# A row gradient in 32 tiles: every third store moved to Pool's DMA queue, in two halves

## The chip, the core and the metric

The kernel runs on one core of a Trainium2 chip. The metric is the device time in microseconds (us) of one execution; the profile's span, from the first to the last instruction, is a little shorter. Of the core's engines the kernel uses VectorE (DVE in the profile), GpSimd (POOL), and SyncE (SP) for issuing DMA transfers. The core has 16 DMA engines, which carry out all transfers between the main memory (DRAM) and the on-chip memory with its 128 partitions (SBUF).

## The reference

```python
def reference(x: np.ndarray) -> np.ndarray:
    return np.gradient(x, axis=1)
```

x is 8192 x 8192 in float32, 268.4 MB, and so is the output. Inside a row the gradient is half the difference of the right and the left neighbour; the first element is x[1] - x[0] and the last is x[-1] - x[-2].

## The kernel before

A tile is 256 rows: 128 partitions with R = 2 rows each, so one partition holds 64 KB that lie together in DRAM, and a tile is 8.39 MB. There are 32 tiles. NB = 3 slots in SBUF hold one tile each; tile i lives in slot i % 3. A slot has SH = 64 spare columns at its front: the load (line 60) puts the tile behind them, and the result is written into the same slot 64 columns further to the front, so that no second buffer is needed.

Per tile the steps are:

1. The load, on SP's queue (line 60). From the fourth tile on it waits until the store of the tile that had the slot before has landed.
2. Pool takes the differences at both ends of each row into `ends` (line 70). It waits for the load.
3. VectorE works out the inside of both rows in one custom instruction, half the difference of two shifted views (line 81). It waits for step 2. The last tile is done in two pieces.
4. The end values are copied over the row ends of the result (line 92), by VectorE, or by Pool for tiles with i % 5 equal to 1 or 3.
5. The store, on SP's queue (line 94). It waits for step 4.

The order on each engine is written by hand (`manual_schedule`), and every engine works through its own list in order. SP's list is: loads of tiles 0 to 2; then, for each group of three tiles, their three stores and after them the three loads of the next group. A wait at the head of SP's list therefore holds up all that stands behind it. The helper `chain` names for each instruction the steps that it has to wait for; `stores[i]` is what the load of tile i + 3 waits for:

```python
ins = nc.sync.dma_start(out=b[:, SH : SH + W], in_=x_sets[i])
loads.append(chain(i, ins, *([stores[i - NB]] if i >= NB else [])))
```

Of the kernel before, what the change touches and what calls it, by code (L numbers as in the profile page):

```python
# [1 line left out]

# [4 lines left out]


@with_exitstack
def kernel(  # L10
    ctx: ExitStack,
    tc: tile.TileContext,
    x: bass.AP,
    out: bass.AP,
):

    nc = tc.nc
    P = nc.NUM_PARTITIONS
    n, m = x.shape
    R = 2
    NB = 3  # L30
    SH = 64
    W = R * m
    nsets = n // (P * R)
    f32 = x.dtype

    x_sets = x.rearrange("(s p t) m -> s p (t m)", p=P, t=R)
    out_sets = out.rearrange("(s p t) m -> s p (t m)", p=P, t=R)

    pool = ctx.enter_context(tc.tile_pool(name="pool", bufs=1))
    slots = [pool.tile([P, SH + W], f32, name=f"slot{k}", tag=f"slot{k}") for k in range(NB)]  # L40
    ends = pool.tile([P, nsets, R, 2], f32, name="ends", tag="ends")
    loads, stores = [], [None] * nsets
    in_front = {}

    def chain(i, ins, *needed):

        group, engine = f"slot{i % NB}", ins.ins.engine
        keep = [o.ins for o in needed]  # L50
        if in_front.get(engine, (None,))[0] == group:
            keep.append(in_front[engine][1])
        tc.declare_no_dep(ins.ins, group=group, keep=keep, reason="implied by the needed step")
        tc.add_to_no_dep_group(group, ins.ins)
        in_front[engine] = group, ins.ins
        return ins

    def load(i):
        b = slots[i % NB]
        ins = nc.sync.dma_start(out=b[:, SH : SH + W], in_=x_sets[i])  # L60
        loads.append(chain(i, ins, *([stores[i - NB]] if i >= NB else [])))

    with tc.manual_schedule():
        for i in range(NB):
            load(i)
        for i in range(nsets):
            b = slots[i % NB]
            xin = b[:, SH : SH + W].rearrange("p (t m) -> p t m", m=m)

            ins = nc.gpsimd.tensor_sub(  # L70
                out=ends[:, i, :, :],
                in0=xin[:, :, 1 : m : m - 2],
                in1=xin[:, :, 0 : m - 1 : m - 2],
            )
            at = [chain(i, ins, loads[i])]
            last = i == nsets - 1
            nr = 1 if last else R
            for r in range(0, R, nr):
                c0, c1 = r * m + 1, (r + nr) * m - 1

                ins = nc.vector._custom_dve(  # L81
                    dve_ops.TENSOR_TENSOR_REDUCE_SUB_MAX,
                    out=b[:, c0:c1],
                    in0=b[:, SH + c0 + 1 : SH + c1 + 1],
                    in1=b[:, SH + c0 - 1 : SH + c1 - 1],
                    s0=0.0,
                    s1=0.5,
                )
                halved = chain(i, ins, *at)
                res = b[:, r * m : (r + nr) * m].rearrange("p (t m) -> p t m", m=m)  # L90
                placer = nc.gpsimd if i % 5 in (1, 3) and not last else nc.vector
                ins = placer.tensor_copy(out=res[:, :, 0 : m : m - 1], in_=ends[:, i, r : r + nr, :])  # L92
                placed = chain(i, ins, halved)
                ins = nc.sync.dma_start(
                    out=out_sets[i, :, r * m : (r + nr) * m], in_=b[:, r * m : (r + nr) * m]
                )
                stores[i] = chain(i, ins, placed)
                at = [halved]
            if i % NB == NB - 1:
                for k in range(i + 1, min(i + 1 + NB, nsets)):  # L100
                    load(k)


# [1 line left out]
_INS = ['x']  # L105
_OUTS = [((8192, 8192), 'float32')]


# [23 lines left out]
```

## Time and profile before

| | before |
|---|---|
| device time, median of 3 runs | 1248.15 us (1247.39 to 1248.5) |
| span of the profiled execution | 1245.0 us |
| VectorE busy | 554.8 us, 45% |
| Pool busy | 8.8 us, 1% |
| moved by DMA | 268.44 MB read, 268.44 MB written |
| mean rate over the span | 431 GB/s |
| one tile on VectorE (line 81), the usual form | 17.22 us |

The profile is a page on one execution. Its strip cuts the span into 40 slices, with a digit for the busy tenths of each engine and of the DMA engines, and the rate in GB/s under it. Its other parts list the DMA queues, with packets, bytes and the share of the 16 engines' time, and the groups of instructions. The trace behind the page answers further questions: a timeline in order of time, in which SPq lines are transfers issued by SP, and tables of waits, where "A <- B: us, times, longest" says that A waited for B.

### The profile page before, as it was taken

To read this page: it belongs to the slowest core of one execution; us is meant where nothing else is said; L and a number is where in the kernel's file an instruction comes from. 1 tells how busy PE (TensorE), PEld (TensorE's weight loads), DVE (VectorE), ACT (ScalarE), POOL (GpSimd) and SP (SyncE) were. 2 spreads that over 40 slices of the span, in tenths; PEclk is the share of its full clock that TensorE was granted. 3 is DMA by queue.
4 is the path that set the end of the run, shared out by engine and by line. 5 is a ranking of instruction groups with operands and counts; after the bars stand their busy time and mean duration, and the time that the engine had idled before them with its cause. 6 is when DMAs were issued, how large, how long until landed. Compare 5 with 4: busy or idle time off the path is not lost.

```text
span 1245.0 us, 241 instructions
## 1 busy us (share of the span) xinstructions
DVE 554.8 (45%) x54; POOL 8.8 (1%) x48
## 2 busy tenths in 40 slices
DVE  2850483079009603850582079009603840591083
POOL 0000000000000000000000000000000000000000
DMA  9999999999999999999999999999999999999999
GB/s 404 438 436 419 425 438 438 438 438 438 434 427 421 436 438 438 436 438 432 432 419 438 436 438 432 436 434 432 423 436 436 436 438 436 430 427 430 436 411 404
DMA packets 9361, 536.88 MB, mean 431 GB/s; under 512 B 1040, under 2 KB 1040, under 8 KB 1040
## 3 DMA queue, kind: packets, MB, share of 16 engines
q1 hardware_dynamic: 9360, 536.88, 99.8%
q14 instruction: 1, 0.01, 0.0%
HBM read 268.44 MB, written 268.44 MB: 431 GB/s over the span
## 4 chain that ended last, share of the span: by engine, by line
another core or an unknown queue 74%; DVE 18%; DMA 3%; issue 2%; POOL 1%; SPq 0%; POOLq 0%
DVE slot L81 18%; DMA slot<-in_x_dram 3%; POOL ends L70 0%; POOL slot L92 0%; SPq L60 0%; DVE slot L92 0%; POOLq L127 0%
## 5 line engine op out<-in xcount | busy, mean ns | idle before, releaser
L81 DVE CUSTOM_DVE_ANT_0 slot<-slot 128x16382 f32<-128x16382 f32 (+1 forms) x33 | 551.3, 16706 | 667.9 <-POOL ends L70 667.9
L70 POOL TENSOR_TENSOR ends<-slot 128x4 f32<-128x4 f32 x32 | 6.3, 198 | 988.8 <-DMA slot<-in_x_dram 988.8
L92 DVE COPY slot<-ends 128x4 f32<-128x4 f32 (+1 forms) x21 | 3.6, 172 | 0.7
L92 POOL COPY slot<-ends 128x4 f32<-128x4 f32 x12 | 2.3, 190 | 207.9 <-DVE slot L81 207.9
L116 POOL MEMSET const-bfloat16-1.0<- 128x1 bf16 x1 | 0.1, 102 | 0.0
L116 POOL MEMSET const-uint8-127<- 128x1 uint8 x1 | 0.1, 102 | 0.0
L116 POOL MEMSET const-float32-0.0<- 128x1 f32 x1 | 0.1, 99 | 0.2 <-issue 0.2
L116 POOL MEMSET const-float32-1.0<- 128x1 f32 x1 | 0.1, 99 | 0.0
## 6 DMA issues: line engine op xcount, KB each, us to landing
out_dram<-slot SPq DMA_DIRECT2D x2, 4096.0 KB, 20.2
slot<-in_x_dram SPq DMA_DIRECT2D x32, 58.0
out_dram<-slot SPq DMA_DIRECT2D x31, 40.3
```

Of the source, the lines that this page charges most:

```text
L70: ins = nc.gpsimd.tensor_sub(out=ends[:, i, :, :], in0=xin[:, :, 1 : m : m - 2], in1=xin[:, :, 0 : m - 1 : m - 2],)
L81: ins = nc.vector._custom_dve(dve_ops.TENSOR_TENSOR_REDUCE_SUB_MAX, out=b[:, c0:c1], in0=b[:, SH + c0 + 1 : SH + c1 + 1], in1=b[:, SH + c0 ...
L92: ins = placer.tensor_copy(out=res[:, :, 0 : m : m - 1], in_=ends[:, i, r : r + nr, :])
L116: nc = _bacc.Bacc("TRN2", target_bir_lowering=False, num_devices=1)
```

## The change

The stores of tiles with i % 3 equal to 2 (tiles 2, 5, ... 29, ten of them) leave SP's queue. Pool issues each of them as two transfers: the tile's partitions 0 to 63, and its partitions 64 to 127. On the DRAM side the 64 blocks of a half are written as 8 times 8[...]. The load that next uses the slot waits for both halves. SP's list then has, for each group, two stores and three loads. The purpose is that SP does not hold the next loads behind the third store, and that loads and the third store stand in different queues.

```diff
-    loads, stores = [], [None] * nsets
+    loads, stores = [], [[] for _ in range(nsets)]
...
-        loads.append(chain(i, ins, *([stores[i - NB]] if i >= NB else [])))
+        loads.append(chain(i, ins, *(stores[i - NB] if i >= NB else [])))
...
                 placed = chain(i, ins, halved)
+                if i % NB == NB - 1:
+
+                    for h in range(2):
+                        rows = out_sets[i, 64 * h : 64 * h + 64, :].rearrange("(a c) w -> a c w", a=8)
+                        ins = nc.gpsimd.dma_start(out=rows, in_=b[64 * h : 64 * h + 64, 0:W])
+                        stores[i].append(chain(i, ins, placed))
+                    at = [halved]
+                    continue
                 ins = nc.sync.dma_start(
                     out=out_sets[i, :, r * m : (r + nr) * m], in_=b[:, r * m : (r + nr) * m]
                 )
-                stores[i] = chain(i, ins, placed)
+                stores[i].append(chain(i, ins, placed))
```

## The prediction

> **What bounds the kernel now.** I read the strip of the span first, then the table of DMA queues, the time to landing, the waits of SP, and last the timeline of one group of three tiles. The strip and the queue table, from the page:
>
> ```profile
> DVE  2850483079009603850582079009603840591083
> POOL 0000000000000000000000000000000000000000
> DMA  9999999999999999999999999999999999999999
> GB/s 404 438 436 419 425 438 438 438 438 438 434 427 421 436 438 438 436 438 432 432 419 438 436 438 432 436 434 432 423 436 436 436 438 436 430 427 430 436 411 404
> ...
> q1 hardware_dynamic: 9360, 536.88, 99.8%
> ```
>
> Every slice has the DMA engines at nine tenths or more; the one queue in use keeps all 16 engines at work for 99.8% of the span. 0.998 x 16 x 1245.0 = 19,880 engine-us carry 536.88 MB, so one engine moves 27.0 GB/s. VectorE has holes of whole slices, Pool is hardly there: neither is the bound. Now the timeline of tiles 5 and 6 (start, duration, what, in brackets the idle time before and who ended it):
>
> ```profile
> 139.84 0.20 POOL L70 TENSOR_TENSOR ends<-slot 128x4 f32<-128x4 f32 x1 [77.19 <-DMA slot<-in_x_dram]
> ...
> 157.57 38.99 SPq L94 DMA_DIRECT2D out_dram<-slot  x3
> 159.18 0.20 POOL L70 TENSOR_TENSOR ends<-slot 128x4 f32<-128x4 f32 x1 [1.64 <-DMA slot<-in_x_dram]
> ...
> 178.54 0.20 POOL L70 TENSOR_TENSOR ends<-slot 128x4 f32<-128x4 f32 x1 [19.16 <-DMA slot<-in_x_dram]
> 178.78 17.22 DVE L81 CUSTOM_DVE_ANT_0 slot<-slot 128x16382 f32<-128x16382 f32 x1 [1.93 <-POOL ends L70]
> 196.03 0.17 DVE L92 COPY slot<-ends 128x4 f32<-128x4 f32 x1
> 197.84 39.18 SPq L60 DMA_DIRECT2D slot<-in_x_dram  x3
> 255.87 0.20 POOL L70 TENSOR_TENSOR ends<-slot 128x4 f32<-128x4 f32 x1 [77.13 <-DMA slot<-in_x_dram]
> 256.10 17.22 DVE L81 CUSTOM_DVE_ANT_0 slot<-slot 128x16382 f32<-128x16382 f32 x1 [59.90 <-POOL ends L70]
> ```
>
> Line 70 starts when a load has landed. Loads land at 139.84, 159.18 and 178.54, so one transfer of 8.39 MB takes 19.35 us; a group (three loads, three stores) takes 255.87 - 139.84 = 116.03 = 6 x 19.34. There are 64 transfers: 64 x 19.35 = 1238.4 us, and the span is 1245.0. Only 6.6 us, 0.5%, lie above a DMA that never pauses, and a part of that is the start and the last landing. The waits of SP:
>
> ```profile
> SPq L94 <- DVE slot L92: 525.7, 21, 55.9
> SPq L60 <- DMA out_dram<-slot: 373.2, 29, 19.2
> SPq L94 <- POOL slot L92: 298.8, 12, 36.7
> ```
>
> SP waits a lot, but always with work queued behind it: load 6, issued at 197.84, lands at 255.80, which is three transfers later, so two stores stood before it. None of those waits costs time.
>
> [...]
>
> **The change part by part.** Tiles 2, 5, ... 29 are concerned: 10 of 32 stores, 83.9 MB.
>
> *Removed*: ten store issues on SP, and with them SP's wait for the third tile. Store 5 was issued at about 196.2 and store 3 landed at about 197.8 (that is when load 6 goes out), so load 6 still waits for store 3 and goes out at the same time: 0.
>
> *Added*: twenty issues on Pool. No row shows one. From below, the cost is Pool's own short operation, 0.20 us[...]. Behind them on Pool stands line 70 of the next tile, due at 255.87; VectorE behind it has idled for 59.90 us. The engines meanwhile have store 4, 19.35 us, on SP's queue. Cost 0 in either bound.
>
> *The wait of the third load*: it now needs both halves. If the halves share the engines evenly with store 4, both stores end at about 197.5 + 2 x 19.35 = 236.2. Load 7 goes out then and not at 217, load 8 right behind. Load 6 has been queued since 197.84 and keeps the engines until 255.5, so 19 us of slack: 0.
>
> *Which partitions an engine reads*: this is where I see a cost. [...] a Pool share of eight rows (8 x 2.42 = 19.35 us of one engine) takes 38.7 us. Three orders give the same sum: store 4 first and then the Pool store (19.35 + 38.7); row by row in turn (8 x (2.42 + 4.84)); or both at once with equal bytes[...] (2 x 19.35 x 1.5). All are 58.05 us where there were 38.7, so +19.35 us a group, and the DMA is the bound, so nothing hides it. Ten groups: +193.5 us. From below it is 0[...].
>
> Sum: 1248.15 + 193.5 = 1441.7, with 1248.15 at the other end.
>
> **The rivals.**
> *Partial sharing*: the pairs drift apart, or an engine uses the time on its other queue. At half the loss, +97: 1345, anywhere from 1270 to 1425. For it: rows of store 4 and of Pool's run mixed. [...]
> *No difference*: the shares don't collide. The bytes and the engines' rate are the same, so 1248. For it: the 99.8% and 64 x 19.35; nothing that the change takes off SP was on the path. [...]
> *A gap at each turn*: the second half waits for the first, or load 8 comes late, and engines go dry [...]. Against: the 19 us of slack.
> *Faster, the other side*: two queues per engine hide the pauses between transfers. All that there is to win is 6.6 us in the profile, and the first and the last slice, at 404 GB/s beside 438, hold (1 - 404/438) x 31.1 = 2.4 us each of start and end. With half of it gone, 1248.15 - 3.3 = 1244.9. For it: slices of 419 to 427 GB/s beside 438. Against: the group of 116.03 us shown is already six full transfers.
>
> **How the numbers follow.** Full sharing 0.40, partial 0.15, a gap 0.10, no difference 0.28, faster 0.07. The prediction is the likeliest, 1441.7 us, rounded to 1441. The range has to hold the case without a difference too: from 1246.5, which leaves out the faster case and the lower edge of no difference, to 1446, full sharing with 4 us of the small gaps. That makes faster 0.07, same 0.28, slower 0.40 + 0.15 + 0.10 = 0.65.
>
> **What would show each step.** Right: the second queue appears with 83.9 MB, the DMA strip stays at nine while GB/s falls to about two thirds of 435 (some 290) over some 58 us in each group, and the load after a third store lands 97 instead of 77 us after the load before it; the group is 135.4 us. Wrong: GB/s near 436 throughout and groups of 116 us (no sharing); GB/s of 436 with dips and the DMA below nine (gaps). If Pool's line 70 or VectorE start later than a load's landing by more than 0.2 us, my zero for Pool's issue falls. The prediction falls as a whole if an engine's share isn't eight consecutive partitions[...].

## The result and the profile after

The changed kernel takes 1419.72 us (1416.08 to 1429.57, 4 runs), the kernel before 1248.33 us beside it. The ratio is 1.139, with a 95% interval of 1.133 to 1.145: 13.9% slower. The prediction was 1441 us. Throughout, ratios and their intervals leave out executions more than 1.5% slower than the fastest of the same kernel; medians and ranges hold all.

The page of the changed kernel, the strip and the DMA queues:

```profile
DMA  9999999999999999999999999999999999999959
GB/s 415 415 356 285 436 432 319 324 437 430 319 358 430 434 297 393 426 393 323 397 408 345 361 424 397 326 382 412 443 326 400 432 369 356 417 402 360 380 235 391
...
q1 hardware_dynamic: 7920, 452.99, 76.9%
q0 software_dynamic: 1600, 83.89, 20.5%
```

The DMA engines are as busy as before, slice by slice, but for one slice near the end. Yet in every group there is a hole in the rate, to 285 to 360 GB/s in the slices shown, and to 235 in that late slice. The second queue, q0, is Pool's. It moves 15.6% of the bytes and holds the engines for 21% of their busy time. One 64 KB row costs an engine 0.205 x 16 x 1414.2 / 1280 = 3.62 us on Pool's queue; before, it cost 19,880 / 8192 = 2.43 us (a tile is 128 such rows, so ten stores are 1280 and 64 transfers 8192).

The timeline of the group that answers to the one shown of before (Pool's line 71 starts when a load has landed):

```profile
199.31 0.20 POOL L71 TENSOR_TENSOR ends<-slot 128x4 f32<-128x4 f32 x1 [19.14 <-DMA slot<-in_x_dram]
199.55 17.22 DVE L82 CUSTOM_DVE_ANT_0 slot<-slot 128x16382 f32<-128x16382 f32 x1 [1.91 <-POOL ends L71]
216.80 0.17 DVE L93 COPY slot<-ends 128x4 f32<-128x4 f32 x1
217.27 1.09 POOL L99 DMA_DIRECT2D out_dram<-slot  x2 [17.76 <-DVE slot L93]
218.60 67.73 SPq L61 DMA_DIRECT2D slot<-in_x_dram  x3
300.54 0.19 POOL L71 TENSOR_TENSOR ends<-slot 128x4 f32<-128x4 f32 x1 [82.18 <-DMA slot<-in_x_dram]
300.77 17.22 DVE L82 CUSTOM_DVE_ANT_0 slot<-slot 128x16382 f32<-128x16382 f32 x1 [83.79 <-POOL ends L71]
```

The next load lands 101 us after the third load, where it was 77 us. Pool's two issues take 1.09 us in a stretch in which Pool and VectorE then idle for over 80 us. Within that stretch, in windows of 10 us (start:end, length, VectorE and Pool busy, clock, DMA share, GB/s; the share is the busy part of the 16 engines, and passes 1 because a row counts whole in the window in which it begins):

```profile
199.00:219.00 20.00, 17.39 (x2) 1.29 (x3) 1.00 1.01 436
219.00:229.00 10.00, 0.00 (x0) 0.00 (x0) 1.00 1.08 334
229.00:239.00 10.00, 0.00 (x0) 0.00 (x0) 1.00 1.02 256
239.00:249.00 10.00, 0.00 (x0) 0.00 (x0) 1.00 0.98 262
249.00:259.00 10.00, 0.00 (x0) 0.00 (x0) 1.00 1.00 315
259.00:269.00 10.00, 0.00 (x0) 0.00 (x0) 1.00 0.99 282
269.00:279.00 10.00, 0.00 (x0) 0.00 (x0) 1.00 0.96 380
279.00:289.00 10.00, 0.00 (x0) 0.00 (x0) 1.00 1.00 433
```

From the issue on Pool the rate falls from 436 to between 256 and 380 GB/s for some 60 us, at a DMA share near 1.00. The engines work all the time and move less. The ten groups take 127 to 140 us, where they took 116 to 117.

A part of the loss is idle time of the DMA engines. SP's waits first:

```profile
SPq L61 <- DMA out_dram<-slot: 809.0, 29, 54.0
```

Loads wait 809 us for stores instead of 373. That alone costs nothing as long as the engines have other work, as in the windows above, where the share is 0.96 or more. Where they run dry, the share falls. In the end stretch, the same columns:

```profile
1344.00:1355.00 11.00, 0.00 (x0) 0.00 (x0) 1.00 0.80 346
1355.00:1365.00 10.00, 9.47 (x1) 0.19 (x1) 1.00 0.18 79
1365.00:1375.00 10.00, 8.10 (x3) 0.20 (x1) 1.00 0.35 151
```

A share of 0.18 is three of 16 engines, and the packets' records of the trace have three rows under way there. Those few are still bringing in the last load while the others have run out of work: 2.2 + 8.2 + 6.5 = 16.9 us idle at the end. The accounts from the two pages: engines busy 97.4% of 1414.2 = 1377.4 us against 99.8% of 1245.0 = 1242.5, so +134.9 us of slower transfers; idle 36.8 against 2.5, so +34.3 us; together the 169.2 us of the span.

### The profile page after: what moved, and what is told of

Its sections match the earlier page's. It is cut to its first block, busy times and chain, and to the rows that moved or that the text cites. A ratio compares the mean times of both kernels' runs of the same rounds, so it can differ in the third digit from the quotient of the medians.

```text
span 1414.2 us, 269 instructions
## 1 busy us (share of the span) xinstructions
DVE 554.8 (39%) x54; POOL 19.8 (1%) x68
## 3 DMA queue, kind: packets, MB, share of 16 engines
q1 hardware_dynamic: 7920, 452.99, 76.9%
q0 software_dynamic: 1600, 83.89, 20.5%
## 4 chain that ended last, share of the span: by engine, by line
another core or an unknown queue 47%; DMA 33%; DVE 15%; issue 3%; POOL 1%; SPq 0%; POOLq 0%
DMA slot<-in_x_dram 18%; DVE slot L82 15%; DMA out_dram<-slot 14%; POOL out_dram L99 0%; POOL ends L71 0%; SPq L61 0%; DVE slot L93 0%; POOL slot L93 0%; POOLq L136 0%; POOLq L99 0%
## 5 line engine op out<-in xcount | busy, mean ns | idle before, releaser
L99 POOL DMA_DIRECT2D out_dram<-slot x20 | 11.0, 553 | 107.8 <-DVE slot L93 106.6
## 6 DMA issues: line engine op xcount, KB each, us to landing
out_dram<-slot SPq DMA_DIRECT2D x2, 4096.0 KB, 20.2
```

What stands on the lines that cost most here:

```text
L99: ins = nc.gpsimd.dma_start(out=rows, in_=b[64 * h : 64 * h + 64, 0:W])
```

## The experiments

The theory was port sharing: I supposed that some partitions share a way for DMA, a port in my word, and that two engines at work on such partitions get half the rate each. That was my estimate; no trace shows a port, and the runs can only show which partitions slow each other. Rival 1: Pool's queue, or having two queues on an engine, is slow in itself. Rival 2: two smaller transfers in place of one, or transfers on eight engines, are the cost.

**Quarters in two orders.** The store as four transfers, in two orders for which port sharing expected different times:

```diff
-                    for h in range(2):
-                        rows = out_sets[i, 64 * h : 64 * h + 64, :].rearrange("(a c) w -> a c w", a=8)
+                    for p in (0, 64, 32, 96):   # the other kernel: (0, 32, 64, 96)
+                        rows = out_sets[i, p : p + 32, :].rearrange("(a c) w -> a c w", a=8)
...
```

> The same stores of tiles 2, 5, ... 29 on Pool's queue, but as four transfers of 32 partitions[...], in the order 0, 64, 32, 96. [...] Port sharing (my theory): [...] 1248 to 1255 us. Rival 1, Pool's queue or a second queue on an engine is slow in itself: 1420 or more. Rival 2, transfers on eight engines each with more completions are the cost: 1420 or more, since there are twice as many.

> The same four transfers as in the run with quarters in the order 0, 64, 32, 96, only in the order 0, 32, 64, 96: the transfers of partitions 0 to 31 and 32 to 63 run together [...]. Port sharing: [...] about 1420 us, at most 1441. Rivals 1 and 2: the same time as with the other order, whatever it is, since number, size, queue and engines of the transfers are the same.

Measured: 1408.63 us (1391.91 to 1416.1) and 1407.74 us (1404.17 to 1446.15). My theory expected 1248 to 1255 for the first and missed it by over 150 us; the outcome is the one that rivals 1 and 2 expected. Either sharing is not the cause, or the engines do not get the partitions that I supposed.

**The whole store on Pool's queue.** One transfer of 128 partitions:

```diff
-                    for h in range(2):
...
+                    ins = nc.gpsimd.dma_start(out=out_sets[i], in_=b[:, 0:W])
+                    stores[i].append(chain(i, ins, placed))
```

> The third store on Pool's queue as one transfer of 128 partitions. Port sharing: 1248 to 1252 us [...]; about 1420 if it deals out eight consecutive partitions. Rival 1 (Pool's queue, or two queues on an engine): 1420. Rival 2 (eight engines per transfer): 1248.

Measured: 1271.82 us (1262.46 to 1290.55), 1.2% to 2.1% slower than before. Rival 1 expected 1420: Pool's queue has a price, 15 to 26 us by this interval, but not 171. My own 1248 to 1252 took no such price into account and missed too.

**Only the last tile's store.**

```diff
-                if i % NB == NB - 1:
+                if last:
...
```

> Only the store of the last tile is changed: its two pieces of one row each go on Pool's queue in halves of 64 partitions [...]; all else is as before. They run with at most the end of the store of tile 30 beside them. Port sharing: the last tile's 8.39 MB take 38.7 instead of 19.35 us, and nothing follows, so 1248.2 + 19.4 = 1267.6 us. Two queues running beside each other as the cause (rival 1 in its second form): about 1248 to 1251.

Measured: 1267.58 us (1267.19 to 1268.2), +19.5 us, as computed. Both pieces are issued by 1226; the windows from there on:

```profile
1234.00:1244.00 10.00, 0.00 (x0) 0.00 (x0) 1.00 0.94 210
1244.00:1254.00 10.00, 0.00 (x0) 0.00 (x0) 1.00 0.93 226
```

SP's queue has nothing left, and the engines move 210 to 226 GB/s at a share of 0.93 to 0.94. So it is not two queues that slow each other; the halves are slow alone. Nor are they crowded onto eight engines while eight rest: the share would then be 0.5.

**Why the quarters failed.** The built program has no 8 times 8. Neighbouring blocks of equal step have been folded: a half has one count of 64 on the DRAM side and one on the SBUF side, a quarter one count of 32. That the 8 would give a half to eight engines was my supposition, and the trace of the changed kernel speaks against it. In the first of Pool's stores the packets' records have 64 rows begun from 85.58 to 108.50 us, then 16 completion records from 114.00 to 116.18, and the next row at 116.42. So in this store the halves ran one after the other, and up to 16 rows of the first were under way at once. At one row to an engine, as in the kernel before (16 rows under way for 97% of its time), that is twice what eight engines hold. If folded quarters are spread over the engines in the same way, their order can't help; for them this is an estimate. The next runs test the rest.

**Halves on SP's queue, neighbouring or even and odd.** Neither Pool's queue nor a second queue takes part:

```diff
-                        ins = nc.gpsimd.dma_start(out=rows, in_=b[64 * h : 64 * h + 64, 0:W])
+                        ins = nc.sync.dma_start(out=out_sets[i, 64 * h : 64 * h + 64, :], in_=b[64 * h : 64 * h + 64, 0:W])
+                        # the other kernel: out_sets[i, h : P : 2, :] and b[h : P : 2, 0:W]
```

> The third store in the two halves of 64 neighbouring partitions, but on SP's queue: no second queue, nothing from Pool. Port sharing: [...] each such store takes 38.7 instead of 19.35 us: 1248.2 + 10 x 19.35 = 1441.7 us[...]. Rival 1 (Pool's queue or a second queue): 1248 to 1251 us.

> As the halves on SP's queue, but one transfer takes the 64 even and the other the 64 odd partitions: same size, same number of transfers[...]. Port sharing: 1248 to 1252 us[...]. Rival 2 (two transfers of 64 partitions in place of one of 128 are the cost): the same as the neighbouring halves on SP's queue.

Measured: neighbouring halves 1445.79 us (1423.37 to 1464.22), even and odd 1247.73 us (1246.66 to 1248.88), beside 1247.52 us of the kernel before. The ratio of the first is 1.146, interval 1.140 to 1.151, that of the latter 1.000, interval 0.999 to 1.001. Two windows inside one store of the neighbouring halves, and the queue of that run:

```profile
240.00:250.00 10.00, 0.00 (x0) 0.00 (x0) 1.00 1.03 210
260.00:270.00 10.00, 0.00 (x0) 0.00 (x0) 1.00 0.94 197
...
q1 hardware_dynamic: 9520, 536.88, 97.7%
```

Even and odd:

```profile
GB/s 404 437 437 435 425 418 437 437 437 437 435 437 431 431 427 427 437 437 435 437 435 433 433 433 429 427 437 437 436 433 433 433 437 435 427 423 435 437 385 404
...
q1 hardware_dynamic: 9520, 536.88, 99.7%
```

Rival 1 falls as the main cause: without Pool, the loss is all there, 175 to 189 us by the interval. Rival 2 falls in its first form: two transfers of 64 partitions cost nothing here if one has the even and the other the odd ones (1247.73 beside 1247.52 us).

**The change with even and odd partitions.** The same edit on Pool's queue:

> The change itself with even and odd partitions in place of the lower and upper 64: Pool's queue, two transfers, the same waits. Port sharing: what the whole store on Pool's queue took, 1262 to 1291 us, so the sharing is some 145 of the change's 171 us. If the two transfers or Pool's queue were the cost, 1420 us.

Measured: 1265.24 us (1255.9 to 1273.18), +17.7 us. Its profile, of an execution with a span of 1254.0 us, has no holes but for the slices at the end:

```profile
GB/s 403 433 435 435 435 435 435 435 435 433 435 433 435 429 429 435 418 435 435 435 435 435 431 435 435 435 429 431 435 429 435 433 435 414 435 433 431 429 324 401
...
q0 software_dynamic: 1600, 83.89, 15.5%
```

A row on Pool's queue costs 0.155 x 16 x 1254.0 / 1280 = 2.43 us, as before the change. Of the change's 171 us, which partitions go together makes some 154.

**Rows in an order that can't be folded.** Here against the folded quarters (the run with halves does the same to the halves of the change). The third tiles' rows then land in another order in DRAM; the bytes are the same, 83.89 MB on Pool's queue:

```diff
-                        rows = out_sets[i, p : p + 32, :].rearrange("(a c) w -> a c w", a=8)
+                        rows = out_sets[i, p : p + 32, :].rearrange("(c a) w -> a c w", a=8)
```

> In the change as compiled, the 8 times 8 on the DRAM side has been folded into 64 even blocks[...]. Here the rows of each half are written in another order, which can't be folded (the third tiles' rows end up permuted within a half, so that part of the output is changed)[...]. Port sharing as predicted [...]: about 1420 us, as the change. If eight engines with eight partitions each do not share: 1255 to 1275 us.

> Quarters of 32 partitions [...], in the order 0, 64, 32, 96, with rows in an order that can't be folded (again the third tiles' rows are permuted, within a quarter). [...] Port sharing: what Pool's queue takes without sharing, 1255 to 1291 us. Rival 2 (small transfers): 1410 us or more, as the folded quarters took.

> The same quarters in the order 0, 32, 64, 96: partitions 0 to 31 and 32 to 63 run together [...]. Port sharing: 1400 to 1446 us. If the order of the quarters makes no difference, the time of the other order.

In the built program the DRAM side of a quarter now keeps its 8 and 4. Measured: halves 1462.98 us (1439.86 to 1469.82, ratio to before 1.162, interval 1.152 to 1.172); quarters in the order 0, 64, 32, 96 1255.48 us (1252.54 to 1258.39, ratio 1.005); in the order 0, 32, 64, 96 1403.52 us (1383.52 to 1407.92, ratio 1.119). The last two differ in nothing but the order of four transfers, and by 148 us. The rate and Pool's queue, first of the order 0, 64, 32, 96:

```profile
GB/s 405 430 434 434 434 434 434 432 432 434 434 432 434 434 421 413 436 434 426 419 430 434 434 432 434 430 434 417 436 430 421 413 434 434 434 434 434 419 403 369
...
q0 software_dynamic: 3200, 83.89, 15.6%
```

And of the order 0, 32, 64, 96:

```profile
GB/s 418 418 418 343 416 420 358 410 423 438 343 356 420 403 352 367 421 384 375 360 410 388 382 308 437 380 343 362 418 381 306 416 403 373 330 418 401 373 216 390
...
q0 software_dynamic: 3200, 83.89, 16.8%
```

The first is as flat as before the change, the second has the holes. Port sharing expected this; rival 2 in its second form (small transfers) expected 1410 us or more for the first and falls. The four runs also show that the folding counts: folded, the order makes no difference (1408.63 and 1407.74); unfolded, it decides (1255.48 and 1403.52).

One rival has no run of its own. The upper 64 partitions of a tile are also the upper 4 MB of its stretch in DRAM, so every split above is a split of DRAM addresses too. If a stretch of DRAM were the limit, I would expect all rows in it to be slow alike. The packets' records of the changed kernel speak against it: while two of Pool's rows, begun at 1295.95 and 1296.62 us, took 6.37 and 6.75 us, twelve others, begun between 1298.90 and 1300.10, took 2.42 us each. This is one place in one trace and not an experiment; that the limit goes with the partitions, and not with the DRAM side, is supported but not shown apart.

**Loads in halves.** The stores as before, the third load of each group in two transfers of 64 partitions:

```diff
-        ins = nc.sync.dma_start(out=b[:, SH : SH + W], in_=x_sets[i])
...
+        for p in (0, 64) if i % NB == NB - 1 else (0,):
+            e = p + 64 if i % NB == NB - 1 else P
+            ins = nc.sync.dma_start(out=b[p:e, SH : SH + W], in_=x_sets[i, p:e, :])
...
```

> The stores are as before; the loads of tiles 2, 5, ... 29 go on SP's queue in two transfers of 64 neighbouring partitions. If a port is limited in the same way when it is written, 1248.2 + 10 x 19.35 = 1441.7 us; if only reads of the on-chip memory share, 1248 to 1252 us.

Measured: 1539.45 us (1535.31 to 1544.46), +292 us, more than the 193.5 expected. The timeline shows the landing of the second and of the third load of a group (Pool's line 73 starts when a load has landed), and two windows lie in the load in halves between them:

```profile
180.20 0.20 POOL L73 TENSOR_TENSOR ends<-slot 128x4 f32<-128x4 f32 x1 [2.48 <-DMA slot<-in_x_dram]
220.45 0.20 POOL L73 TENSOR_TENSOR ends<-slot 128x4 f32<-128x4 f32 x1 [40.05 <-DMA slot<-in_x_dram]
...
180.00:190.00 10.00, 9.57 (x1) 0.20 (x1) 1.00 1.02 210
190.00:200.00 10.00, 7.83 (x2) 0.00 (x0) 1.00 1.00 210
```

Writing is slowed in the same way: 210 GB/s. The group from 160.01 to 297.49 us takes 137.5 us, 21 more than before; but the groups grow, and the one from 999.89 to 1149.78 takes 149.9 us. The growth lies between the landings of the first and the second load of a group, both whole loads, which are 20.2 us apart in the first of these groups (160.01 and 180.20) and 36.1 in the other (999.89 and 1036.00). Why was not tried and stays open.

## Why the prediction was right, and where it was not

*What bounds the kernel*: right. The DMA engines had no slack (99.8% busy before), and longer rows turned into a longer span: 134.9 of its 169.2 us.

*The zeros for SP's removed issues and Pool's added ones*: right. Line 99 takes 1.09 us for two, and at 300.54 Pool's line 71 and at 300.77 VectorE start at once after the load.

*Which partitions an engine reads*: right in that the rows of a half slow each other, wrong in its working. I took an engine's share to be eight consecutive partitions on eight engines, and two such engines to get one engine's rate between them; both were my suppositions, and no trace of the kernel before shows either. In the changed kernel's trace up to 16 rows of a half are under way at once. The prediction named another share as a sign by which it would fall as a whole, and as far as that trace shows it, the step failed. That its sum held none the less is luck: neighbouring halves alone move at 210 to 226 GB/s at a DMA share of 0.93 to 0.94, about half of the 431 before, with the rows spread otherwise than I supposed. The order of rows that can't be folded, meant to give the eights that I supposed, costs more than the change (1.162 against 1.139), and more than the 1420 us that I expected of it; why was not tried. What the runs show of the partitions is this: 64 neighbouring ones move at 197 to 226 GB/s in the windows shown of the halves, and with 64 even and 64 odd ones the rate is 418 GB/s or more in all but three of the 40 slices. Nor does the full rate need one transfer of 128 partitions: even and odd ones take 1247.73 us, and quarters in the order 0, 64, 32, 96 take 1255.48 if they are not folded.

*The size, +193.5 us*: of the right order, but too large. Longer transfers made 134.9 us, and 39 of these fall on SP's own rows (76.9% of the span, or 2.52 us a row). The signs that the prediction named came near: the load after a third store lands 88 to 101 us after the one before (97 forecast), groups take 127 to 140 us (135.4 forecast). But the holes run at 256 to 380 GB/s, not at a steady 290, and the rows on Pool's queue took 3.62 us on average and not 4.84. The packets' records show how: of the 1280 rows, 518 took under 2.5 us, as before the change, and 384 took 4.5 us or more. So sharing was partial, as in the rival of that name, and the measured time lies in the range given to it (1270 to 1425). That it is partial because the engines that share drift apart was only argued. Without the second queue the total came out nearer, 1445.79 us against 1441.7, but its executions range from 1423 to 1464, and in its profile, too, the loss is made of both parts: 97.7% of 1454.1 us busy, so +178.2 us of longer transfers and +30.9 of idle time.

*The wait of the third load, 0*: the zero stands. In the group shown, the third load went out at about 286 us (218.60 + 67.73), 14 us before the first load of its group landed at 300.5; in the nine groups with a third load this slack is 9.7 to 14.5 us, where 19 were forecast. What the prediction left out is that the engines do not advance alike. Idle time grew by 34.3 us, 16.9 of it at the end, where three engines finished a load alone. Between 853 and 859 us, too, the DMA share is 0.33, though the third load had gone out at about 826: the engines that were ahead had run dry, and the next store went out only at 858.2. The two errors, 134.9 - 193.5 = -58.6 and +34.3, have opposite signs and sum to -24.3 us in the span; the device time came out 21 us under the 1441 predicted. That it came within 1.5% is thus in part luck, and the range, from no difference to full sharing, left room for most cases.

*The rivals*: no difference and faster are excluded by the interval; partial sharing fits best. Gaps exist, as the idle time, but half of it lies at the end and not at the turns. Pool's queue without sharing costs 0.5% to 1.6% (1255.48, 1265.24, 1271.82; ratios 1.005, 1.014, 1.016). Why these three differ, and what of it is drift between engines, stays open.

No version beat the kernel before; even and odd halves on SP's queue equal it.

## What to carry to other kernels

In a kernel bound by DMA, a split by partitions can cost half the rate, so measure the rate of the partitions that are at work at one time. Even and odd partitions on one queue cost nothing here (1247.73), while the lower and the upper 64 move at 210 GB/s where the mean before is 431. Quarters in the order 0, 64, 32, 96 cost next to nothing (1255.48), but only with their rows in the order that can't be folded: the same order, folded, took 1408.63. A DMA share near 1.00 does not say that the engines are at their rate (1.03 stood beside 210 GB/s in the halves on SP's queue); read the GB/s beside it. And look at the built program before trusting a split of dimensions in the source, since here equal steps were folded.

## What was not expected of the hardware

A transfer in neighbouring halves can take a little more than twice as long. The load in halves shown above landed 40.25 us after the load before it (180.20 to 220.45), where a whole one takes 19.35, which is 2.08 times. In the halves on SP's queue, the window from 240 to 250 us has 210 GB/s, which is 32 rows, at a share of 1.03, so a row costs about 1.03 x 16 x 10.00 / 32 = 5.15 us, where it cost 2.43 before. The runs with a second queue and an even rate were not free either: at 2.43 us a row (even and odd) and 0.156 x 16 x 1256.4 / 1280 = 2.45 us (quarters in the order 0, 64, 32, 96) they took 1.4% and 0.5% longer. And the size of the damage varies from execution to execution far more than that of the kernel before: 1423 to 1464 us for the halves on SP's queue, 1246.61 to 1248.62 for the kernel before beside them.
